# One recurrence head's norm: token sums in nine columns, one small root, and rows made by a product with the identity

## The chip, the cores and the metric

The kernel runs on one core of one Trainium2 chip. The metric is the device time of one launch in microseconds (us). A core has five engines that run their own instruction lists and wait for each other by semaphores: TensorE (PE, with its weight loads PEld), VectorE (DVE), ScalarE (ACT), GpSimd (POOL) and SyncE (SP, which here only issues transfers).

## The reference, cut to what matters

One layer of a hybrid decoder over 1024 prompt tokens and 64 sample tokens. Three head groups read the same normalised input. The change is in group B, a gated linear recurrence with four heads of 128 value features. After the recurrence each token's 128 values of a head are divided by their root mean square, and then gated:

```python
o, S = hgrn2_scan(q, k, v, log_f, S0)            # o: (B, L, 4 heads, 128)
o = o * lax.rsqrt(jnp.mean(o * o, axis=-1, keepdims=True) + EPS)
o = o.reshape(B, L, HGRN_WIDTH) * onorm_g * jax.nn.silu(g)
```

So the norm needs one number for each of 1088 tokens and 4 heads: 4352 inverse roots.

## The kernel before, in words

Activations lie feature by feature: a tile has 128 features on the partitions and the 1088 tokens (1024 prompt, 64 sample) along the free axis. Tokens are cut into three slices `CH` of 364, 362 and 362 columns. Large products are made of three passes over split operands (lines 282 to 284: high part by high, high by low, low by high). They are called projection products here; eight input tiles make 24 of them for one slice of one output tile, and `project` yields after each 6.

The input projections are cut in seven groups (`FIRST`, `WIN[0]` to `WIN[5]`). From `WIN[0]` on, `weave` runs a group's projection steps and, between them, the steps of one head's recurrence, the generator `hgrn(h)`: while the projections for head h+1 stand on PE, head h is worked off. `weave` is told how many steps a head has (`HS`), and spreads so many over the group. With head 3 the cross-attention (`xattn`) and after it the pooling mixer (`pool_mix`) are woven in too. The order in which instructions stand on an engine is then made by a scheduler from the program's order, the pools' free buffers and its own estimates.

The pools matter here: `bank(...)` takes one of four PSUM banks, `tmp(...)` one of seven scratch tiles, `hrow` one of nine half rows.

In `hgrn(h)` the norm stands behind the head's output `o` (line 781; lines 789 and 791 make it, line 798 the 64 sample columns, ACT copies at lines 792 and 800). For each slice (lines 803 to 813): ACT squares it (line 807), a product with a matrix of ones (line 809) sums over the 128 partitions and gives the same sum on each of them, so that the result is already a row by token, equal on all partitions. Then `rsqrt` works on the whole 128x364 tile: mean plus EPS (line 256), an integer shift and subtraction for a first guess (lines 258, 259) and three Newton steps, each a square on ACT (line 250) and two DVE instructions (lines 251, 252). Line 812 multiplies `o` by it. Behind the norm, line 822 makes the sample states' update (`Us`), and line 824 writes them out; then `g_evac` gates `o` (lines 832 to 836).

The kernel has small roots elsewhere. `token_sums` (line 293) takes 128 tokens as the stationary operand, in four strips of 32 columns side by side, and one column of ones as the moving one, so that the sums stand by token on the partitions, in one column. `rstd_last` (line 314) brings such a column back to a row: the column, repeated 128 times, is the stationary operand, and the identity the moving one (line 334).

After these stages come the output projection (lines 953 to 955), the up projection with the convolution (lines 1230 to 1232) and the down projection (lines 1381 to 1383).

Of the kernel before, what the change touches and what calls it, by code (L numbers as in the profile page):

```python
# [15 lines left out]
ALU = mybir.AluOpType  # L16
# [14 lines left out]
CH = [(0, 364), (364, 726), (726, 1088)]  # L31
# [19 lines left out]
def trunk(ctx, tc, I, O):  # L51
# [21 lines left out]
    mm = nc.tensor.matmul  # L73
    act = nc.scalar.activation
    tt = nc.vector.tensor_tensor
# [3 lines left out]
    def row(name, cols=1106, p=128):  # L79
        return rowp.tile([p, cols], F32, tag="row", name=name, bufs=RB)  # L80
# [4 lines left out]
    def tmp(name, cols=None, dt=F32):  # L85
        return now["wk"].tile([128, cols or now["cols"]], dt, tag="tmp", name=name, bufs=now["tmps"])
# [4 lines left out]
    def work(name, tag, bufs, cols, dt=F32):  # L91
        return now["wk"].tile([128, cols], dt, tag=tag, name=name, bufs=bufs)

    def bank(name, shape):
        if now["name"] == "down":
            return acc(name, shape)
        return now["psB"].tile(shape, F32, tag="b", name=name)

    def acc(name, shape):
        return now["psA"].tile(shape, F32, tag="a", name=name)  # L100
# [67 lines left out]
    ident = cst[:, C_ID:C_ID + 128]  # L168
    ones = cst[:, C_ONE:C_ONE + 128]
# [76 lines left out]
    def newton(y, v, a, small):  # L246
        if small:
            tt(out=a, in0=y, in1=y, op=ALU.mult)
        else:
            act(out=a, in_=y, func=AF.Square)  # L250
        stt(out=a, in0=a, scalar=-0.5, in1=v, op0=ALU.mult, op1=ALU.mult)
        stt(out=y, in0=a, scalar=1.5, in1=y, op0=ALU.add, op1=ALU.mult)


    def rsqrt(ss, dim, y, v, a, small=False):
        ts(out=v, in0=ss, scalar1=1.0 / dim, scalar2=EPS, op0=ALU.mult, op1=ALU.add)
        yi = y.bitcast(I32)
        ts(out=yi, in0=v.bitcast(I32), scalar1=1, scalar2=None, op0=ALU.logical_shift_right)
        ts(out=yi, in0=yi, scalar1=-1.0, scalar2=MAGIC, op0=ALU.mult, op1=ALU.add)
        for _ in range(3):  # L260
            newton(y, v, a, small)
# [31 lines left out]
    def token_sums(out, x, start=True, stop=True):  # L293

        for c in range(0, 128, 32):
            mm(out[c:c + 32], x[:, c:c + 32], ones[:, 0:1], start=start, stop=stop, tile_position=(0, c))
# [122 lines left out]
    def head_rows(h):  # L419
        if h not in FR:  # L420
            FR[h], KR[h] = row(f"f{h}", NT), row(f"K{h}", NT)
        QR[h], VR[h] = row(f"Q{h}", NT), row(f"V{h}", NT)
# [4 lines left out]
    for c in range(3):  # L427
        a, b = CH[c]
# [251 lines left out]
    def hgrn(h):  # L680
        f, K, Q, V = FR[h], KR[h], QR[h], VR[h]
# [13 lines left out]
        for half in range(2):  # L695
            tp = bank(f"vtp{h}{half}", [128, 4, 128])
            for i in range(4):
                n = 4 * half + i
# [9 lines left out]
        for li, b in enumerate(LEVELS):  # L708
# [12 lines left out]
            else:  # L721
                nj = 64 // b
                ps = bank(f"sc{h}_{b}", [128, 8, b])
                for n in range(8):
                    for j in range(nj):
                        s0 = 2 * j * b
                        mm(ps[s0:s0 + b, n, :], K[:, n * 128 + s0:n * 128 + s0 + b], Qo[:, n, j, :],
                           start=True, stop=True)
# [8 lines left out]
            if b == 16:  # L737
                for j in range(4):
                    c = slice(32 * j, 32 * j + 32)
# [13 lines left out]
        for hf in range(2):  # L753
            Kt = hrow(f"Kt{h}{hf}").rearrange("p (n v) -> p n v", n=4)
            tp = bank(f"ktp{h}{hf}", [128, 4, 128])
            for i in range(4):
                n = 4 * hf + i
# [7 lines left out]
            for i in range(4):  # L765
                n = 4 * hf + i
# [14 lines left out]
        o = row(f"o{h}", NT)  # L781
# [3 lines left out]
        for hf in range(2):  # L785
            ps = bank(f"o{h}{hf}", [128, 4, 128])
            for i in range(4):
                n = 4 * hf + i
# [7 lines left out]
        for b in range(8):  # L796
            for c in range(0, 128, 32):
                mm(ps[c:c + 32, b, :], s0[b // 4][:, b % 4, c:c + 32], Q[:, NP + 8 * b:NP + 8 * b + 8],
                   start=False, stop=True, skip_group_check=True, tile_position=(0, c))
        act(out=o[:, NP:NT], in_=ps, func=AF.Copy)  # L800
        yield

        for c in range(3):
            a, b = CH[c]
            n = b - a
            sq = tmp(f"osq{h}{c}")
            act(out=sq[:, 0:n], in_=o[:, a:b], func=AF.Square)
            ss = bank(f"oss{h}{c}", [128, n])
            mm(ss, ones, sq[:, 0:n], start=True, stop=True)
            y, v, t = tmp(f"oy{h}{c}"), tmp(f"ov{h}{c}"), tmp(f"ot{h}{c}")  # L810
            rsqrt(ss, 128, y[:, 0:n], v[:, 0:n], t[:, 0:n])
            tt(out=o[:, a:b], in0=o[:, a:b], in1=y[:, 0:n], op=ALU.mult)
            yield

        for hf in range(2):
# [42 lines left out]
    def units(lst, chunk_major=False):  # L858
# [4 lines left out]
        return [lambda nm=nm, j=j, c=c: project(nm, j, c, EV[nm](j)) for nm, j, c in o]  # L863

    hg = [hgrn(h) for h in range(4)]
    HS, XS, PS = 20, 31, 9
    head_rows(1)
    FR[2], KR[2] = row("f2", NT), row("K2", NT)
    weave(units(WIN[0]), (hg[0], HS))
# [727 lines left out]
    a, b = NQ, 2 * NQ  # L1597
# [84 lines left out]
def build(arrays):  # L1682
    nc = bacc.Bacc("TRN2", target_bir_lowering=False, num_devices=1)
    I = {k: nc.dram_tensor(f"in_{k}", a.shape, mybir.dt.from_np(a.dtype), kind="ExternalInput").ap()
         for k, a in arrays.items()}
    O = {k: nc.dram_tensor(f"out_{k}", s, F32, kind="ExternalOutput").ap() for k, s in OUTS.items()}
    with tile.TileContext(nc) as tc:
        with ExitStack() as ctx:
            trunk(ctx, tc, I, O)
    return nc  # L1690
# [27 lines left out]
```

## Time and profile before

| what | value |
|---|---|
| median of 3 runs | 1228.74 us (1227.69 to 1230.68) |
| the profiled execution, its own time | 1228.64 us |
| its span, first to last instruction | 1226.9 us |
| PE busy in the span | 1192.4 us (97%) |
| DVE busy | 925.3 us (75%) |
| ACT busy | 545.4 us (44%) |
| POOL busy | 260.9 us (21%) |

The span is the part that the trace shows; 1.7 us of the execution's time lie around it. A matrix product of the program that is not split by hand appears as two PE records (two passes), a transpose as one. PE's records are pipelined and overlap: a record of 0.33 us is followed by the next after 0.17 us, so the cost of a product is read from start to start. A busy PE is PE with something in flight, not PE at its peak. [...] `q8 instruction` in the table of transfer queues are loads of instructions.

### The profile page before, as it was taken

What the parts mean: (1) busy time and instruction counts of PE and PEld (TensorE: products, weight loads), DVE (VectorE), ACT (ScalarE), POOL (GpSimd) and SP (SyncE); (2) the same over time, 40 slices, a digit from 0 to 9 for tenths busy, and PEclk for the clock granted to TensorE, in tenths of its full rate; (3) what the DMA queues carried; (4) which work ended last, traced back from release to release, by engine and by line L of the source; (5) the groups of instructions that cost most, each with busy time, mean ns of one, the idle gap of its engine ahead of it and who ended that gap; (6) DMA issues with size and microseconds to landing.
All of it is one profiled execution on the core that took longest, in us unless ns stands there. A gap on an engine that the chain in (4) does not pass through costs nothing.

```text
span 1226.9 us, 27524 instructions
## 1 busy us (share of the span) xinstructions
PE 1192.4 (97%) x11332; PEld 1148.2 (94%) x11332; DVE 925.3 (75%) x1675; ACT 545.4 (44%) x1044; POOL 260.9 (21%) x297
## 2 busy tenths in 40 slices
PE   6999999999999999899999999999999999999996
PEld 6999898978878899899999999999999999999996
DVE  7685869487877458989779878987786969868534
ACT  7743534223455455743333332333333445554542
POOL 0000000000000001445454554544323000100242
PEclk9999999999999999999999999999999999999998
DMA  8031111223102643213454354344212597345333
GB/s 270 27 121 53 37 53 53 78 79 120 39 23 91 236 135 115 89 61 132 146 191 139 107 173 159 119 157 158 89 53 70 190 333 263 90 128 151 96 97 111
DMA packets 75838, 148.20 MB, mean 121 GB/s; under 512 B 9264, under 2 KB 31280, under 8 KB 75712
## 3 DMA queue, kind: packets, MB, share of 16 engines
q1 hardware_dynamic: 71776, 140.73, 34.9%
q0 software_dynamic: 1568, 5.39, 1.2%
q8 instruction: 89, 1.46, 0.5%
q10 hardware_dynamic: 2368, 0.32, 0.2%
q14 instruction: 37, 0.30, 0.1%
HBM read 110.48 MB, written 35.93 MB: 119 GB/s over the span
## 4 chain that ended last, share of the span: by engine, by line
PE 59%; DVE 8%; issue 3%; ACT 1%; POOL 0%; DVEq 0%; ACTq 0%; POOLq 0%
PE po L955 2%; PE po L953 2%; PE po L954 2%; PE uUa L1232 2%; PE pV L1381 2%; PE pV L1382 2%; PE pV L1383 2%; PE uUa L1230 2%; PE pP L1381 2%; PE pP L1382 2%; PE uUa L1231 2%; PE uPa L1232 2%; PE pP L1383 2%; PE pU L1381 2%; PE uPa L1230 2%
## 5 line engine op out<-in xcount | busy, mean ns | idle before, releaser
L1369 DVE TENSOR_TENSOR dlp<-drp,dhp 128x512 fp32r<-128x512 f32 x77 | 54.2, 712 | 35.3 <-ACT dhp L1368 34.3
L1368 ACT ACTIVATE dhp<-drp 128x512 fp32r<-128x512 f32 x77 | 47.7, 626 | 69.8 <-PE pU L1382 21.2
L1348 DVE TENSOR_TENSOR xop<-B,xop 128x544 fp32r<-128x544 f32 x70 | 50.0, 729 | 11.6 <-ACT xop L1374 11.6
L1374 ACT ACTIVATE xop<-B 128x544 fp32r<-128x544 f32 x70 | 43.9, 648 | 25.1 <-DVE xop L1348 13.0
L1381 PE MATMUL pU<-xop,dhp 128*128 128x272 f32 x176 | 50.8, 288 | 0.1
L1382 PE MATMUL pU<-xop,dhp 128*128 128x272 f32 x176 | 50.7, 288 | 0.0
L1382 PE MATMUL pV<-xop,dhp 128*128 128x272 f32 x176 | 50.7, 288 | 0.0
L1381 PE MATMUL pV<-xop,dhp 128*128 128x272 f32 x176 | 50.6, 288 | 0.0
L1383 PE MATMUL pV<-xop,dlp 128*128 128x272 f32 x176 | 50.6, 287 | 0.0
L1383 PE MATMUL pU<-xop,dlp 128*128 128x272 f32 x176 | 50.5, 287 | 0.0
L1193 DVE TENSOR_TENSOR g<-g,uc 128x272 f32<-128x272 f32 x66 | 46.1, 699 | 0.8
L1263 ACT ACTIVATE g<-g 128x1104 f32<-128x1104 f32 x22 | 24.8, 1128 | 40.8 <-DVE g L1262 40.8
L1260 DVE SCALAR_TENSOR_TENSOR g<-a,vec,g 128x1104 f32<-128x1104 f32 x22 | 31.8, 1444 | 14.5 <-ACT g L1258 14.5
L1166 POOL TENSOR_TENSOR us0a<-ura 128x512 f32<-128x512 f32 x11 | 18.9, 1718 | 106.3 <-DVE ow160l L925 86.5
L1381 PE MATMUL pP<-xop,dhp 128*128 128x272 f32 x144 | 41.4, 288 | 0.0
L1382 PE MATMUL pP<-xop,dhp 128*128 128x272 f32 x144 | 41.4, 288 | 0.0
L1383 PE MATMUL pP<-xop,dlp 128*128 128x272 f32 x144 | 41.4, 287 | 0.0
L1262 DVE SCALAR_TENSOR_TENSOR g<-a,vec,g 128x1104 f32<-128x1104 f32 x22 | 39.6, 1802 | 0.0
L1266 DVE TENSOR_TENSOR g<-g,ra 128x560 f32<-128x560 f32 x22 | 36.9, 1676 | 0.0
L824 POOL DMA_DIRECT2D out_sstate<-s x8 | 4.3, 541 | 139.9 <-DVE s L823 139.9
L1381 PEld LDWEIGHTS pU<-xop,dhp 128*128 128x128 f32 x176 | 33.1, 188 | 0.3 <-DVE xd L1500 0.3
L1383 PEld LDWEIGHTS pU<-xop,dlp 128*128 128x128 f32 x176 | 33.2, 188 | 0.0
(2313 smaller groups left out, 5053.5 us busy)
## 6 DMA issues: line engine op xcount, KB each, us to landing
ds<-in_wdown SPq DMA_DIRECT2D x44, 256.0 KB, 3.1
ura<-in_wup SPq DMA_DIRECT2D x22, 512.0 KB, 4.4
urb<-in_wup SPq DMA_DIRECT2D x22, 512.0 KB, 3.5
sd<-ds SPq DMA_DIRECT2D x44, 256.0 KB, 2.0
drp<-sd SPq DMA_DIRECT2D x44, 256.0 KB, 2.8
fd<-g SPq DMA_DIRECT2D x20, 544.0 KB, 3.9
B<-fd SPq DMA_DIRECT2D x40, 272.0 KB, 5.6
drp<-in_wdown SPq DMA_DIRECT2D x33, 256.0 KB, 3.2
```

What stands on the lines that cost most here:

```text
L1193: tt(out=dst, in0=dst, in1=s_, op=ALU.mult)
L1230: mm(ps, wh[:, w], xh[:, k], start=first and k == 0, stop=False, skip_group_check=True)
L1232: mm(ps, wl[:, w], xh[:, k], start=False, stop=k == 3, skip_group_check=True)
L1262: stt(out=cw[:, 0:1104], in0=aw[:, 0:1104], scalar=col(V_CW, 3 * f), in1=cw[:, 0:1104], op0=ALU.mult, op1=ALU.add)
L1266: tt(out=tail, in0=tail, in1=ra[0], op=ALU.mult)
L1348: tt(out=out, in0=in0, in1=in1, op=ALU.subtract)
L1368: act(out=wh, in_=raw, func=AF.Copy)
L1369: tt(out=wl, in0=raw, in1=wh.bitcast(F32), op=ALU.subtract)
L1374: act(out=t[:, 0], in_=x, func=AF.Copy)
L1381: mm(ps, w[0][:, c], h, start=start, stop=False, skip_group_check=True)
L1382: mm(ps, w[0][:, c], l, start=False, stop=False, skip_group_check=True)
L1383: mm(ps, w[1][:, c], h, start=False, stop=stop, skip_group_check=True)
```

## The change

The three slices' squares stay on ACT. Their sums are taken by `token_sums`: nine groups of 128 tokens (three to a slice, the last of each overlapping the one before), each one column of a 128x9 PSUM tile. One `rsqrt` with `small=True` then runs on 128x9 for the whole head: twelve DVE instructions, the Newton squares among them (line 248), and none on ACT. Three products per slice, with the repeated column as the stationary and the identity as the moving operand, put the roots back as a row over the tokens, now in PSUM, and the multiplication reads them there. The generator has two more yields, and `HS` goes from 20 to 22.

```diff
@@ -800,16 +800,27 @@
         act(out=o[:, NP:NT], in_=ps, func=AF.Copy)
         yield
 
+        ss = bank(f"oss{h}", [128, 9])
         for c in range(3):
             a, b = CH[c]
             n = b - a
             sq = tmp(f"osq{h}{c}")
             act(out=sq[:, 0:n], in_=o[:, a:b], func=AF.Square)
-            ss = bank(f"oss{h}{c}", [128, n])
-            mm(ss, ones, sq[:, 0:n], start=True, stop=True)
-            y, v, t = tmp(f"oy{h}{c}"), tmp(f"ov{h}{c}"), tmp(f"ot{h}{c}")
-            rsqrt(ss, 128, y[:, 0:n], v[:, 0:n], t[:, 0:n])
-            tt(out=o[:, a:b], in0=o[:, a:b], in1=y[:, 0:n], op=ALU.mult)
+            for i, t in enumerate((0, 128, n - 128)):
+                token_sums(ss[:, 3 * c + i:3 * c + i + 1], sq[:, t:t + 128])
+        y, v, t = [work(f"o{i}{h}", "head", 3, 9) for i in "yvt"]
+        yield
+        rsqrt(ss, 128, y, v, t, small=True)
+        yield
+        for c in range(3):
+            a, b = CH[c]
+            n = b - a
+            yb = bank(f"ob{h}{c}", [128, n])
+            for i, t in enumerate((0, 128, n - 128)):
+                lo = 128 * i
+                mm(yb[:, lo:t + 128], y[:, 3 * c + i:3 * c + i + 1].to_broadcast([128, 128]), ident[:, lo - t:128],
+                   start=True, stop=True)
+            tt(out=o[:, a:b], in0=o[:, a:b], in1=yb, op=ALU.mult)
             yield
 
         for hf in range(2):
@@ -863,7 +874,7 @@
-    HS, XS, PS = 20, 31, 9
+    HS, XS, PS = 22, 31, 9
```

The functions that it calls are in the kernel already:

```python
def token_sums(out, x, start=True, stop=True):
    for c in range(0, 128, 32):
        mm(out[c:c + 32], x[:, c:c + 32], ones[:, 0:1], start=start, stop=stop, tile_position=(0, c))
```

On every engine the instructions stand as before up to the first head's recurrence and from the output projection on; between them they are moved. SP's list changes by the places of six issues, POOL's not at all. Three places follow. In the rows, a name is the tile, with a number for the buffer, and `x12` counts equal rows that follow each other. Lines behind the change are 11 higher in the changed kernel (833 is 822, 831 is 820).

The first is DVE in head 0, from the arrival of the first sums. Before (`ov`, `oy`, `ot` are the root's tiles, `f<-pf` the evacuation of the next head's projection):

```order
L256 TENSOR_SCALAR ov_1591<-oss_1588 128x364
L258 TENSOR_SCALAR oy_1590<-ov_1591 128x364
L259 TENSOR_SCALAR oy_1590<-oy_1590 128x364
L401 TENSOR_TENSOR f_960<-pf_1532,R_128 128x364
L251 SCALAR_TENSOR_TENSOR ot_1592<-ot_1592,ov_1591 128x364
L252 SCALAR_TENSOR_TENSOR oy_1590<-ot_1592,oy_1590 128x364
L256 TENSOR_SCALAR ov_1629<-oss_1626 128x362
```

And now:

```order
L401 TENSOR_TENSOR f_960<-pf_1486,R_128 128x364
L256 TENSOR_SCALAR ov_1611<-oss_1567 128x9
L258 TENSOR_SCALAR oy_1610<-ov_1611 128x9
L259 TENSOR_SCALAR oy_1610<-oy_1610 128x9
L248 TENSOR_TENSOR ot_1612<-oy_1610 128x9
L251 SCALAR_TENSOR_TENSOR ot_1612<-ot_1612,ov_1611 128x9
L252 SCALAR_TENSOR_TENSOR oy_1610<-ot_1612,oy_1610 128x9
L248 TENSOR_TENSOR ot_1612<-oy_1610 128x9
```

The wide root, which stood between other work slice by slice, has become one chain of narrow instructions behind the evacuation of a projection slice. On PE in this place, the sums stand 6 projection products behind the sample columns of line 798, the first identity products 24 projection products behind the sums.

The second is PE in head 3, where the attention's sample products (`so`, line 614) and the sample columns (`os`, line 798) come together with the norm. Before:

```order
L798 MATMUL os_3950<-Q_2444,s_30_3867 32x8 x9
L614 MATMUL so<-spT,svt_3914 32x16 x16
L798 MATMUL os_3950<-Q_2444,s_30_3867 32x8 x7
L798 MATMUL os_3950<-Q_2444,s_31_3868 32x8 x16
L614 MATMUL so<-spT,svt_3985 32x16 x16
L809 MATMUL oss_4012<-osq_4010,cst 128x364
L614 MATMUL so<-spT,svt_4030 32x16 x16
L284 MATMUL pg_4003<-h4h,wlo_3263 128x362
```

And now:

```order
L798 MATMUL os_3953<-Q_2470,s_30_3899 32x8 x9
L614 MATMUL so<-spT,svt_3929 32x16 x16
L798 MATMUL os_3953<-Q_2470,s_30_3899 32x8 x7
L798 MATMUL os_3953<-Q_2470,s_31_3900 32x8 x16
L614 MATMUL so<-spT,svt_3988 32x16 x16
L296 MATMUL oss_4012<-cst,osq_4013 32x1 x12
L296 MATMUL oss_4012<-cst,osq_4027 32x1 x12
L296 MATMUL oss_4012<-cst,osq_4041 32x1 x12
L614 MATMUL so<-spT,svt_4082 32x16 x16
L284 MATMUL pg_4100<-h3h,wlo_3302 128x362
L614 MATMUL so<-spT,svt_4112 32x16 x16
L282 MATMUL pg_4100<-h4h,whi_3301 128x362
```

All 36 sums stand in a run of small products, with no projection product between line 798 and them. The identity products of head 3 follow 20 projection products and these last two groups of `so` later.

The third is PE a little later, at the first scores of the attention (`xs`) and the first transposes of its probabilities (`xtp`, from `xp`). In the kernel before, 36 projection products (`pu`) stand between the last of the first eight `xs` and the first `xtp`. Now there are 11, of which these are the last four, and all eight transposes stand together:

```order
L284 MATMUL pu_4242<-h4h,wlo_3808 128x364
L282 MATMUL pu_4242<-h5h,whi_3807 128x364
L283 MATMUL pu_4242<-h5l,whi_3807 128x364
L284 MATMUL pu_4242<-h5h,wlo_3808 128x364
L647 MATMUL xtp_4270<-cst,xp_4182 128x128 x4
L647 MATMUL xtp_4276<-cst,xp_4183 128x128 x4
L282 MATMUL pu_4242<-h6h,whi_3807 128x364
```

The first probabilities are asked for 25 projection products sooner.

## Rows read from the trace of the kernel before

**Rows 1.** The page, part 1: busy time, share, instructions.
```profile
PE 1192.4 (97%) x11332; PEld 1148.2 (94%) x11332; DVE 925.3 (75%) x1675; ACT 545.4 (44%) x1044; POOL 260.9 (21%) x297
```

**Rows 2.** Stretches: length, busy PE, PEld, DVE, ACT, POOL; clock, DMA share, GB/s.
```profile
125.00:150.00 25.00, 25.00 (x266) 21.94 (x265) 22.33 (x48) 12.11 (x26) 1.08 (x2) 1.00 0.13 45
```

**Rows 3.** Waits of PE: total us, times, longest (whole span; these lie before 403 us).
```profile
PE po L953 <- DVE sg L835: 1.9, 1, 1.9
PE so L614 <- issue: 1.7, 1, 1.7
...
PE po L955 <- DVE ow000l L925: 0.6, 1, 0.6
...
PE xs L631 <- DVE s L823: 0.2, 1, 0.2
```

**Rows 4.** The wide root by line: ns min/median/max, first and last start.
```profile
L256 DVE TENSOR_SCALAR ov<-oss x12: 525/536/539, 126.9 to 318.8; 128x362 f32<-128x362 f32 x8, 128x364 f32<-128x364 f32 x4
...
L258 DVE TENSOR_SCALAR oy<-ov x12: 340/349/381, 127.4 to 320.3; 128x362 int32<-128x362 int32 x8, 128x364 int32<-128x364 int32 x4
...
L251 DVE SCALAR_TENSOR_TENSOR ot<-ot,ov x36: 522/530/539, 128.7 to 329.0; 128x362 f32<-128x362 f32 x24, 128x364 f32<-128x364 f32 x12
...
L250 ACT ACTIVATE ot<-oy x36: 489/506/511, 128.2 to 328.4; 128x362 f32<-128x362 f32 x24, 128x364 f32<-128x364 f32 x12
```

**Rows 5.** Timeline of PE around two products of line 809: start, us, instruction.
```profile
125.89 0.33 PE L284 MATMUL pf<-h5h,wlo 128*128 128x362 f32 x1
126.06 0.77 PE L809 MATMUL oss<-osq,cst 128*128 128x364 f32 x2
126.39 0.60 PE L282 MATMUL pf<-h6h,whi 128*128 128x362 f32 x1
126.83 0.32 PE L283 MATMUL pf<-h6l,whi 128*128 128x362 f32 x1
...
128.99 0.32 PE L284 MATMUL pf<-h2h,wlo 128*128 128x362 f32 x1
...
130.05 0.33 PE L283 MATMUL pf<-h3l,whi 128*128 128x362 f32 x1
```

**Rows 6.** Timeline of PE, unsplit 128-column products behind each other.
```profile
119.74 0.39 PE L791 MATMUL o<-Q,S 128*128 128x128 f32 x2
119.96 0.39 PE L789 MATMUL o<-scT,Vt 128*128 128x128 f32 x2
```

**Rows 7.** Timeline of PE: token sums of another norm, and what follows.
```profile
56.16 0.37 PE L296 MATMUL n12ss<-cst,n12s 128*32 128x1 f32 x24 [0.34 <-DVE n12s L311]
56.45 0.43 PE L282 MATMUL pi<-h0h,whi 128*128 128x362 f32 x1
56.73 0.33 PE L283 MATMUL pi<-h0l,whi 128*128 128x362 f32 x1
```

**Rows 8.** Timeline of DVE: a Newton step of a small root.
```profile
1218.06 0.16 DVE L248 TENSOR_TENSOR nf10t<-nf10y 128x3 f32<-128x3 f32 x1
1218.26 0.16 DVE L251 SCALAR_TENSOR_TENSOR nf10t<-nf10t,nf10v 128x3 f32<-128x3 f32 x1
```

**Rows 9.** Timeline of ACT at head 3: the copy of the sample columns.
```profile
305.20 0.22 ACT L800 ACTIVATE o<-os 128x64 f32<-128x64 f32 x1 [1.15 <-PE os L798]
```

**Rows 10.** Timeline of DVE: one step of the attention's softmax.
```profile
342.15 0.69 DVE L562 TENSOR_REDUCE x20mx<-xs 128x2 f32<-128x512 f32 x1
...
345.76 0.62 DVE L568 TENSOR_SCALAR xp<-xp,x21sm 128x256 f32<-128x256 f32 x2
```

**Rows 11.** Timeline of PE inside head 3's run of small products.
```profile
304.95 0.38 PE L614 MATMUL so<-spT,svt 128*32 128x16 f32 x21
307.02 0.27 PE L614 MATMUL so<-spT,svt 128*32 128x16 f32 x10 [1.69 <-issue]
```

**Rows 12.** The page, part 3: loads of instructions (packets, MB, share).
```profile
q8 instruction: 89, 1.46, 0.5%
```

**Rows 13.** Stretches behind that wait, columns as in rows 2.
```profile
309.00:311.00 2.00, 2.00 (x7) 2.00 (x8) 1.17 (x4) 1.66 (x6) 0.00 (x0) 0.50 0.34 31
```

## The prediction

> **What bounds the kernel now.** I read the totals first: PE is busy 97% of the span, DVE 75%, ACT 44% [rows 1]. A total says little about one stage, so next come the stretches in which the norm runs. From 125 to 150 us PE is busy all of the time; DVE is busy 22.33 of 25, and much of that is the wide root of head 0 [rows 2]. A busy PE may still be a PE that waits between overlapping records, so third I read start to start: projection products of 362 columns follow each other at 0.17 us on both sides of the norm's products [rows 5], and that is the pace to compare with. Fourth, the waits of PE before 403 us [rows 3]: 1.9 and 0.6 at the start of the output projection, 1.7 inside the attention's sample products, 0.2 at the first scores. No line waits for the root. So in the head stages PE carries the time, and the reader is to see that DVE and ACT run beside it: what the change takes from DVE is worth little, and what it adds to PE is paid.
>
> **What leaves DVE and ACT.** By slice one instruction of 0.536, two of 0.349, six of 0.53, and three ACT squares of 0.506; for twelve slices 6.4 + 8.4 + 38.1 = 53 us of DVE and 18 us of ACT [rows 4]. In come 48 narrow instructions; the nearest, on three columns, last 0.16 [rows 8], so 7.7 us of DVE. The multiplication by a row in PSUM I take at the same cost as before. Net 45 us of DVE. I cost this at nothing: PE's products cover it, and the cover is gone only where PE waits for DVE, which sums to 0.2 us outside the output projection's start [rows 3]. That start hangs on the gating of the last projection slice, whose instructions stand as before.
>
> **What PE pays.** (1) Removed: twelve products of line 809. The first stretches the way from 125.89 to 126.83, in which two projection products would take 0.33, so it costs 0.61; the second, from 128.99 to 130.05, costs 0.73 [rows 5]. Mean 0.67, times twelve 8.0 us, bounds 7.3 and 8.8. (2) Added: three identity products for each slice, 364 columns together. An unsplit product of 128 columns takes 0.22 start to start [rows 6], so 0.63 a slice and 7.5 us in all. The projection product after a change of kind takes 0.28 instead of 0.17 [rows 7]; the removed products have that in their 0.67, so I add 0.11 for each of the ten places where the identity products stand: 8.6 us, bounds 7.5 and 8.9. So the way back to a row costs what the wide sum cost. (3) Added: 36 sums for each head, 72 passes. The same operation in another norm took 0.29 us for 24 passes [rows 7], so 0.87 for a head, 3.5 for four, and 3.9 with four changes of kind. Net of the three: +4.5 us, bounds 2.2 (7.5 + 3.5 - 8.8) and 5.5 (8.9 + 3.9 - 7.3).
>
> [...] Each pass takes 0.29 / 24 = 0.012 us [rows 7]. [...]
>
> **The waits that it moves.** (4) The sums of the third slice need its square, which follows the copy of the sample columns: 0.22 [rows 9] and 0.51 on ACT [rows 4], from the end of line 798. In heads 0 to 2 PE has 6 projection products (1.0) and the sums of two slices (0.58) meanwhile; the 0.85 left covers the handing over, so nothing; without cover 0.7 a head. In head 3 there is no projection product between, and up to 0.5 is lost, but I expect it to fall inside wait (7). What stands behind a PE that waits is the next projection, and nobody else needs that soon. (5) The identity products need the whole chain: twelve narrow instructions at 0.20 start to start [rows 8], 2.4, behind an evacuation of 0.54, so 2.9 against 24 projection products, 4.0. Nothing in heads 0 and 1, and head 2 has as many between. In head 3 the cover is 20 products and two groups of small ones, some 3.9; the chain shares DVE with four wide instructions of other work, some 2.2, so 4.6. I take 0.2 of the 0.7, since the clock may be low there, which lengthens the cover; bounds 0 and 0.7. (6) The first transposes come 25 projection products sooner. Both halves of a softmax step took 4.2 us from the first reduction [rows 10], and one more reduction (0.69) now stands among them: 4.9. The cover is four score products of 256 columns, 1.75 by the rate of [rows 6], eleven projection products, 1.8, and the first half's four transposes, one pass each, 0.45: 4.0. Of the 0.9 I take 0.7, and the old 0.2 at the scores goes away: +0.5, bounds -0.2 and 0.9. (7) In head 3 PE stops for 1.69 us in the middle of a group of equal small products, released by nothing that the profile shows [rows 11]. PE's 22664 records [rows 1] go with 89 instruction loads of 16 KB [rows 12], 255 records to a load, so I read this as a list that ran dry: small products use up a load faster than the next one arrives. The change puts 144 more records (36 sums, two passes, each with a weight load) into just this run. Bounds: nothing, since the position in a load shifts too, and one more stop of 1.7. I take +0.4, near the first, since the stop's length goes by the load's delay and not by the run's.
>
> [...] The rows alone give 255 records a load [rows 1, 12]. [...]
>
> The transfers stay whole; of SP's list six issues change place, with their neighbours. One matters: all loads of the sample values (`svt`) now stand behind the load of `chist`, which waits for head 3's masks. Their first use comes later on PE too, so I take nothing.
>
> **Sum.** 4.5 + 0.2 + 0.5 + 0.4 = 5.6 us on the profiled execution's 1228.64, so 1234.2 us. That execution lies 0.1 below the median shown.
>
> **Rivals.** *A second stop.* [...] With 1.6 for some 3 us of low clock a second stop costs 3.3: 1237.5. For it: 144 records more than before; against it: projection products come right behind. *No measurable change.* The same stop disappears, since the loads' borders shift by 504 records in three heads, and the low clock with it: 0.4 falls away and 3.3 is won, so 1230.5. For it: such a stop is seen at one place alone; against it: head 3's run is longer than a load now, wherever the border falls. *Faster.* PE's full busy share in the head stages hides small waits for DVE that no row names, and 45 us less of DVE takes them away. For it: DVE is near full from 125 to 150 [rows 2]. Against it: the 0.17 start to start next to the norm [rows 5], at which nothing is hidden. It decides from 9.3 us of hidden waits on (5.6 + 3.7); were a quarter of the 45 us on PE's path, 11 us, the time would be 1223. *Dear sums.* The sums cost twice what the other norm's rows show, since they stand among other kinds of product: 3.7 more, 1238. [...]
>
> **How the numbers follow.** The forecast case (1232.5 to 1236.5) has 0.55, the second stop 0.12, the dear sums 0.03, no change 0.25, faster 0.05. 1234.2 is the likeliest case's. The range of 1229.5 to 1238.5 takes in the lost stop, the second one and the dear sums, and leaves out the faster case and some of the edges. 0.3% of the median is 3.7 us, about what a measurement of this kernel can tell from no change; over 1232.4 is slower: 0.55 + 0.12 + 0.03 = 0.70, same 0.25, faster 0.05.
>
> **What would show it.** Line 296 with 288 more passes, at 0.012 us start to start; line 821 with 72 passes, 0.63 us a slice; DVE some 45 us less busy and the span longer all the same; the stop in head 3's small products still there, 1.7 to 2.5 us; a wait of the first `xtp` for the probabilities under 1 us; the wait at the output projection's start unchanged at 1.9. The prediction is wrong if the projection products of the head stages come closer together than 0.17 us over a whole stage, if the stop is gone, or if a wait of several us for the root appears in each head, which would say that a narrow instruction costs far more than 0.20.

## The result and the profile after

The changed kernel takes 1235.11 us (median of 4 runs, 1234.22 to 1236.55), the kernel before beside it 1228.22: a ratio of 1.0053 (95% interval 1.004 to 1.0065). Its profiled execution took 1234.81, with a span of 1233.0. The forecast was 1234.2, slower; the time lies in the range. How it came to 6 or 7 us is not quite how the prediction had it.

The totals of the page after, to be read against [rows 1] and [rows 12]:

```profile
PE 1196.0 (97%) x11668; PEld 1154.0 (94%) x11668; DVE 888.9 (72%) x1615; ACT 530.6 (43%) x1008; POOL 261.4 (21%) x297
...
q8 instruction: 91, 1.49, 0.5%
```

DVE is 36 us less busy, ACT 15, and the kernel is longer. The waits of PE after (total, times, longest), against [rows 3]:

```profile
PE po L966 <- DVE ow170l L936: 2.7, 1, 2.7
PE oss L296 <- issue: 2.1, 1, 2.1
PE po L964 <- ACT ow000h L935: 1.9, 1, 1.9
...
PE po L964 <- ACT ow170h L935: 1.3, 1, 1.3
PE xo L655 <- ACT xt L648: 1.3, 3, 0.8
...
PE po L966 <- DVE ow000l L936: 0.6, 1, 0.6
...
PE xtp L647 <- DVE xp L568: 0.6, 1, 0.6
```

The stop without a releaser is there (2.1, was 1.7), the first transposes wait 0.6, the start of the output projection waits 1.9 and 0.6 as before. New are 1.3 us of `xo` in the attention and, near the end of the output projection, 1.3 of `ow170h` and 0.5 more of `ow170l` (2.2 before), in code that the change doesn't touch.

The sums and the rows on PE in head 0 (timeline: start, us, instruction), against [rows 5]:

```profile
122.27 0.33 PE L284 MATMUL pf<-h7h,wlo 128*128 128x364 f32 x1
122.53 0.78 PE L296 MATMUL oss<-cst,osq 128*32 128x1 f32 x72
123.24 0.43 PE L282 MATMUL pf<-h0h,whi 128*128 128x362 f32 x1
123.51 0.33 PE L283 MATMUL pf<-h0l,whi 128*128 128x362 f32 x1
...
127.17 0.33 PE L284 MATMUL pf<-h7h,wlo 128*128 128x362 f32 x1
127.34 0.81 PE L821 MATMUL ob<-cst,oy 128*128 128x128 f32 x6
127.92 0.41 PE L282 MATMUL pf<-h0h,whi 128*128 128x362 f32 x1
128.17 0.33 PE L283 MATMUL pf<-h0l,whi 128*128 128x362 f32 x1
```

From 122.27 to 123.51 are 1.24 us, of which two projection products would take 0.33: 0.91 for a head's 36 sums. From 127.17 to 128.17, 1.00 less 0.33: 0.67 for a slice's row. A wide sum cost 0.67 in [rows 5].

The next two fences are the timeline of the stop in head 3, and the stretches behind it (columns as in [rows 2]):

```profile
306.21 0.42 PE L296 MATMUL oss<-cst,osq 128*32 128x1 f32 x29
308.72 0.75 PE L296 MATMUL oss<-cst,osq 128*32 128x1 f32 x42 [2.09 <-issue]
```

```profile
308.00:310.00 2.00, 1.28 (x76) 1.24 (x75) 0.44 (x2) 0.34 (x1) 0.00 (x0) 0.50 0.00 0
...
312.00:314.00 2.00, 2.00 (x9) 2.00 (x8) 0.61 (x4) 0.10 (x1) 0.00 (x0) 0.50 0.77 59
```

The stop stands in the middle of the sums, and the granted clock, a share of the full one, is at 0.50 until beyond 314; in [rows 13] it is low too, but from 312 on the kernel before has 1.00. At 0.50 projection products of 362 columns follow each other at 0.30 us (nine from 311.83 to 314.54 in the changed kernel), 1.8 times the 0.17 at 1.00.

**The account.** The table parts each trace in the same way. "Head stages" runs from the 301st projection product (81.4 us before), ahead of any norm, to the first product of the output projection; 1140 projection products at 0.1665 us (189.8) are taken off, and the rest is parted into what PE waited (start to start, 0.1 to 0.2 more for each than the view of waits says), what the low clock cost (start to start, against the same products at full clock), and all other work. "Output" is first to last product of that projection, "rest" from there to the last PE record.

| kernel | head stages | other work | waits | low clock | output | rest |
|---|---|---|---|---|---|---|
| before | 320.2 | 123.5 | 5.0 | 1.9 | 103.4 | 714.4 |
| changed | 324.6 | 125.3 | 6.9 | 2.6 | 107.0 | 713.0 |
| e1 first guess | 316.2 | 122.4 | 4.0 | 0 | 104.9 | 712.9 |
| e2 sums twice | 331.3 | 127.8 | 9.3 | 4.4 | 103.5 | 714.9 |
| e3 rows twice | 331.8 | 132.8 | 7.5 | 1.7 | 103.5 | 715.0 |
| e4 one pass | 317.2 | 118.7 | 6.9 | 1.8 | 106.7 | 714.2 |
| e5 one pass, HS 21 | 312.7 | 120.0 | 2.9 | 0 | 105.4 | 713.4 |
| e6 head 3 old | 318.8 | 126.7 | 2.3 | 0 | 101.8 | 715.3 |
| e7 changed again | 324.2 | 125.3 | 6.6 | 2.5 | 107.0 | 713.2 |
| e8 unsplit sums | 328.1 | 129.7 | 4.6 | 4.0 | 103.3 | 715.2 |
| e9 28 more products | 316.6 | 124.3 | 2.5 | 0 | 107.6 | 714.4 |
| e10 44 more products | 318.4 | 124.6 | 4.0 | 0 | 106.2 | 713.9 |
| e11 changed, HS 20 | 322.3 | 125.9 | 6.6 | 0 | 106.6 | 713.2 |
| e12 changed, 24 more | 324.7 | 125.4 | 7.2 | 2.3 | 106.2 | 713.5 |

So the change is +1.8 of work, +1.9 of waits and +0.7 of low clock in the head stages, and +3.6 - 1.4 behind them. That is 6.6; the spans differ by 6.1, since the time behind PE's last record is 0.5 shorter. e7 repeats it to 0.5. Output and rest are best read as a sum, since a low clock that the kernel before has at the start of the up projection (behind a wait of 1.6 there) comes ahead of that border in the changed one: 817.8 before, 820.0 after. Each trace is one execution: those of e8 and e12 are the slowest of their six (3.4 and 2.3 us above the median), and one run of e4, at 6527 us, is left out of its ratio.

### The profile page after: what moved, and what is told of

It is laid out like the page before. It is cut to its first block, busy times and chain, and to the rows that moved or that the text cites. A ratio compares the mean times of both kernels' runs of the same rounds, so it can differ in the third digit from the quotient of the medians.

```text
span 1233.0 us, 28095 instructions
## 1 busy us (share of the span) xinstructions
PE 1196.0 (97%) x11668; PEld 1154.0 (94%) x11668; DVE 888.9 (72%) x1615; ACT 530.6 (43%) x1008; POOL 261.4 (21%) x297
## 4 chain that ended last, share of the span: by engine, by line
PE 78%; DVE 12%; issue 4%; ACT 3%; DMA 2%; SPq 0%; DVEq 0%; POOL 0%; ACTq 0%; POOLq 0%
PE po L966 2%; PE po L964 2%; PE po L965 2%; PE pP L1392 2%; PE pP L1393 2%; PE pP L1394 2%; PE pU L1392 2%; PE pU L1393 2%; PE pU L1394 2%; PE uPa L1243 2%; PE uVa L1241 2%; PE uPa L1241 2%; PE uUa L1243 2%; PE uPa L1242 2%; PE uUa L1242 2%
## 5 line engine op out<-in xcount | busy, mean ns | idle before, releaser
L213 ACT ACTIVATE whi<-raw 128x1024 fp32r<-128x1024 f32 (+1 forms) x24 | 24.5, 1022 | 38.5 <-PE px L283 14.0
L1392 PEld LDWEIGHTS pV<-xop,dhp 128*128 128x128 f32 x176 | 33.1, 188 | 0.3 <-DVE xd L1511 0.3
```

The costliest lines, as they stand in the source:

```text
L1392: mm(ps, w[0][:, c], h, start=start, stop=False, skip_group_check=True)
```

## The experiments

**What PE is charged: e1 to e3.** e1 takes the relief without the products (`steps` is 0 in `hgrn` and 3 elsewhere):

```diff
-        for _ in range(3):
+        for _ in range(steps):
             newton(y, v, a, small)
```

> The kernel before, with its wide root cut to the first guess: the three Newton steps (36 ACT squares, 72 DVE instructions on 128x362) are left out, so the roots are rough. PE's products stay as they were, all twelve wide sums included; DVE has some 38 us less to do and ACT 18 us less, about the relief that the change brings, without its products. My theory (PE carries the head stages, and DVE and ACT run beside it): 1226 to 1230 us, the projection products still 0.166 to 0.17 apart. Rival (part of DVE's work lies on PE's path unnamed, a quarter of the 56 us): 1213 to 1220 us.

Measured: 1224.93 us, ratio 0.9977 (0.9966 to 0.9987), between the two. The waits of PE up to the output projection's start:

```profile
PE po L953 <- ACT ow000h L924: 1.9, 1, 1.9
PE xo L655 <- ACT xt L648: 1.3, 3, 0.9
...
```

The stop is gone (1.9 from start to start), and with it 1.9 of low clock. The waits of `xo` are new, so that the waits are 1.0 less in all, and the other work is 1.1 less: 4.0 together in the head stages. The run is not the relief alone, since the scheduler moved more than a tenth of PE's records to another place; but 56 us less of DVE and ACT gained 2.9 us in all, the stop and its clock among them. That the stop could vanish with no product removed was unexpected, and e9 takes it up.

e2 and e3 issue the added products twice:

```diff
-                token_sums(ss[:, 3 * c + i:3 * c + i + 1], sq[:, t:t + 128])
+                for _ in range(2):
+                    token_sums(ss[:, 3 * c + i:3 * c + i + 1], sq[:, t:t + 128])
```

> The changed kernel, with every group of token sums issued twice (the second overwrites the first): 288 more passes on PE, nothing else. The changed kernel's 288 passes took 3.0 us without their stop. My theory: +3.0 us, 1238 us; with a further stop for instructions in head 3's run, which grows by 144 more records, up to 1240. [...] Rival that the products added are hidden and the loss comes from the order alone: 1235 us.

> The changed kernel, with every identity product issued twice (the second overwrites the first): 72 more passes on PE, 24 of 362 columns together for each of the twelve slices, nothing else. In the changed kernel a pass of 128 columns takes 0.11 us and the shorter ones 0.09. My theory: +7.5 us (0.63 a slice), 1242.6 us. Rival that the way back to a row is hidden behind other waits of PE: 1235 to 1237 us.

e2: 1239.79 us, 1.0095 (1.0079 to 1.011). Its other work is 2.5 more than the changed kernel's, and head 3 has two stops, shown here; a third, of 1.0 us, stands in head 1's sums at 182 us. The low clock costs 4.4, behind all three:

```profile
PE oss L296 <- issue: 2.6, 1, 2.6
PE so L614 <- issue: 1.6, 1, 1.6
```

e3: 1240.94 us, 1.0108 (1.0095 to 1.0122). Its other work is 7.5 more, as expected; read start to start, the second set costs 0.67 in each of the nine slices of heads 0 to 2, which would be 8.1 for twelve. In both, output and rest together give 1.5 us back, so the times come out below what work and waits add. Nothing of the added products is hidden; the second set of sums costs 2.5 / 288 = 0.009 us a pass.

**A cheaper wide sum: e4 and e5.** The same root, with one pass for its sum:

```diff
-            sq = tmp(f"osq{h}{c}")
+            if h == 0 and c == 0:
+                act(out=onesr, in_=ones[:, 0:2], func=AF.Copy)
+            sq = tmp(f"osq{h}{c}", dt=F32R)
...
-            mm(ss, ones, sq[:, 0:n], start=True, stop=True)
+            mm(ss, onesr[:, 0:1].to_broadcast([128, 128]), sq[:, 0:n], start=True, stop=True)
```

> The kernel before, with the wide root kept and only its sum made cheaper: ACT writes the squares rounded to the operand format of the projection products, and each of the twelve products with the ones is one pass of 362 columns in place of two. My theory (the time goes by PE's products alone): each of the twelve costs 0.17 to 0.28 us in place of 0.67, so 4.7 to 6.0 us less: 1222.2 to 1223.5 us. Rival (the sum on PE is not what counts here, DVE's root is): 1228 us.

1228.94 us, 1.0008 (0.9999 to 1.0018): no gain. Its timeline around a sum:

```profile
126.53 0.33 PE L285 MATMUL pf<-h5h,wlo 128*128 128x362 f32 x1
126.70 0.34 PE L812 MATMUL oss<-osq,onesr 128*128 128x364 f32 x1
126.88 0.33 PE L283 MATMUL pf<-h6h,whi 128*128 128x362 f32 x1
```

The product costs 0.18 here, 0.23 in the mean of eight that stand alone, and the other work is 4.8 less, as the theory has it. But the wait at the output projection's start went from 1.9 to 3.4 and the one behind it from 0.6 to 1.9:

```profile
PE po L956 <- ACT ow000h L927: 3.4, 1, 3.4
...
PE po L958 <- DVE ow000l L928: 1.9, 1, 1.9
```

With the cheaper product the scheduler had moved the eight splits `c` of the output projection's operands: on DVE six of them stand behind the last evacuation `gz` and ahead of the split `ow000l`. Before the first of the eight DVE idles 3.8 us for ACT, but 4.3 in e5 too. In the kernel before none stands there. e5 changes only `HS` to 21, by which two stand there (its expectation says ahead where it should say behind):

> The kernel before with the one-pass sum of e4 and HS at 21, which puts the splits of the output projection's operands behind head 3's gating, nearly as in the kernel before; e4 had them ahead of it. In e4's trace PE's work up to the output projection was 4.8 us shorter than before, and waits and low clock from there on gave 3 to 5 us back. Theory (the saving on PE is real and e4 lost it to the order of the last 20 instructions on DVE and ACT): 1222.5 to 1225 us, with the first wait of the output projection at 1.9 to 2.0 and not 3.5. Rival (the end of the projections is bound by DVE and ACT whatever the order, so PE's saving is lost there): 1228 to 1229 us, and the wait grows by what PE gains.

1221.51 us, 0.9945 (0.9932 to 0.9958), faster than both kernels. The waits up to that start:

```profile
PE po L957 <- DVE sg L839: 1.7, 1, 1.7
PE po L959 <- DVE ow000l L929: 1.1, 1, 1.1
PE so L615 <- issue: 0.4, 1, 0.4
```

Against the kernel before, the gain is 3.5 of work, 1.3 of the stop and the whole of its low clock. The kernel before with `HS` at 21 and the old sum was not run. So it is not shown how the gain divides between the cheaper sum and the new order, nor how much the end of DVE's work would have cost e4 in any order.

**Where the loss sits: e6, e7, e8.** e6 is the changed kernel with the old block under `if h == 3`, and `HS` 20 for that head.

> The changed kernel, with head 3's norm as in the kernel before (HS 20 for it); heads 0 to 2 keep the new norm. Theory (of the loss, head 3's group holds more than its share: the longer stop, its low clock and the waits of the transposes and of the second products of the attention, 3 us more than before; its products cost 0.9 net): against the changed kernel -0.9 for the products, -3.5 for stop, clock and waits, +1.0 because the score products stand among the attention's other products again: 1231.7 us. Rival (each head loses the same by its products, 6.9 / 4): 1233.4 us.

1228.18 us, 0.9991 (0.9981 to 1.0002): three heads of four have the new norm, and the time is that of the kernel before. Its waits from 250 us to the end of the output projection:

```profile
PE po L979 <- DVE ow170l L949: 2.1, 1, 2.1
...
PE xo L655 <- ACT xt L648: 0.2, 1, 0.2
```

The three heads cost 3.2 us of work (three quarters of the 4.5 forecast are 3.4), but no stop is left, and no low clock. So both theories missed: neither had the stop of the kernel before go as well. In this trace the output projection has no low clock either, by which it is 1.6 shorter than before.

e7 is the changed kernel as it is.

> The changed kernel once more, for a second trace and more times. In the first trace the output projection took 107.1 us, in the kernel before 103.5, in e2 and e3, which have the same instructions there, 103.6. If those 3.6 us come of how its transfers happened to fall, the output projection's time will differ from 107.1 in this trace; if the changed kernel has them always, it is 107 again. The time: 1234.5 to 1235.5 us either way.

1234.61 us, 1.0051 (1.0039 to 1.0063); the output projection took 107.0 again. The 3.6 us belong to the kernel.

e8 takes the 128 tokens in one product:

```diff
-                token_sums(ss[:, 3 * c + i:3 * c + i + 1], sq[:, t:t + 128])
+                mm(ss[:, 3 * c + i:3 * c + i + 1], sq[:, t:t + 128], ones[:, 0:1], start=True, stop=True)
```

> The changed kernel with the sums of 128 tokens in one product on all 128 columns in place of four strips of 32: 9 products a head and not 36, the same sums. By the stop's theory (PE's list runs dry because small products use it up faster than it is loaded) head 3's run has 27 products, 108 records, less, and the stop of 2.25 us gets shorter or goes: -1 to -3 us with its low clock. The passes themselves cost between 0.05 and 0.11 us each, 18 a head: 0.9 to 2.0 in place of 0.9. Sum 1232 to 1236 us. Rival (the stop has nothing to do with the number of instructions): the stop stays at 2.2 us, 1235 to 1239 us.

1235.17 us, 1.0057 (1.0042 to 1.0073), no faster than the changed kernel. The stop is gone (a wait of 0.7 for a transfer of `svt` stands near its place), and the sums are dearer: other work is 4.4 more. Head 0, timeline:

```profile
123.82 0.33 PE L284 MATMUL pf<-h7h,wlo 128*128 128x364 f32 x1
123.99 2.06 PE L810 MATMUL oss<-cst,osq 128*128 128x1 f32 x18
125.91 0.41 PE L282 MATMUL pf<-h0h,whi 128*128 128x362 f32 x1
126.16 0.33 PE L283 MATMUL pf<-h0l,whi 128*128 128x362 f32 x1
```

2.34 less 0.33 is 2.01 for 18 passes, 0.11 each against 0.91 / 72 = 0.013 in strips.

**Why the stop comes and goes: e9, e10, e11.** e9 and e10 leave the kernel before as it is, and put products whose result is overwritten ahead of head 0's first sum, 180 us before the stop (seven groups of four in e9, eleven in e10):

```diff
+            if h == 0 and c == 0:
+                for _ in range(7):
+                    token_sums(ss[:, 0:1], sq[:, 0:128])
             mm(ss, ones, sq[:, 0:n], start=True, stop=True)
```

> The kernel before, with 28 more small products (seven groups of token sums, 112 PE instructions) ahead of head 0's first wide sum, which overwrites what they write. Every other instruction on every engine stands as before, and so does head 3's run, some 180 us later. Theory (the stop in head 3 comes where the border of a load of 256 instructions falls, and two loads can't follow each other in less than about 3.5 us): shifted by 112 places no load is used up in less than 3.5 us, so the stop of 1.9 us and the low clock behind it, 1.85, are gone, for 0.7 us of added products: 1225.5 us. Rival (the stop belongs to the run of small products itself, wherever the loads' borders fall): it stays, 1229 us.

> As e9, with 44 more small products (176 PE instructions), the control. Theory: a border now falls so that one load of head 3's run lasts about 2 us, so a stop of 1.5 to 1.9 us stays there with its low clock: 1229 to 1230 us. Rival (any shift or any delay takes the stop away): 1225.7 us.

Waits of PE from 250 to 405 us, e9:

```profile
PE po L956 <- DVE sg L838: 1.9, 1, 1.9
...
PE xs L631 <- DVE s L826: 0.2, 1, 0.2
```

The stop is gone in e9, where on PE nothing differs but the position in the list, and in e10 it is there, with 1.0 us, less than the 1.5 to 1.9 expected, and no low clock behind it. In the trace's records of instruction loads, the loads on either side of the stop begin at 304.65 and 308.27 us in the kernel before, 3.62 apart, and at 306.48 and 310.08 in the changed one, 3.60; nowhere in the fourteen traces do two follow in less than 3.29. So a load that is used up faster stops PE, and whether one is depends on where its border falls in head 3's run.

The traces tie the stops to the loads by two more counts. They have 19 stops without a releaser, of 0.2 to 2.6 us, and each ends 2.2 to 2.9 us after the start of a load. And if all of PE's records (products, weight loads, semaphores) are counted from 0, the one with which PE goes on has in all 19 cases the remainder 193 when divided by 256: 7873 in the kernel before, 8385 in the changed one. The prediction took such a stop for one at a single place. The kernel before has another, in the waits of PE over the whole span:

```profile
PE sc L677 <- issue: 0.5, 1, 0.5
```

It ends at 96.62 us, with record 1729. A run that is longer than a load need not stop, though: e9 has head 3's run and no stop.

The time of e9 is 1229.71 us, though, 1.0016 (1.0007 to 1.0025), not 1225.5: it was 3.8 us ahead at the output projection and lost 4.2 in it, so the rival's 1229 is met for another reason than the rival's. e10: 1228.31, 1.0002 (0.9993 to 1.0011).

> The changed kernel with HS at 20 as before: the same instructions, in another order in the head stages. Counting instructions in loads of 256, head 3's run has one load of 3.1 us in it and none shorter. Theory (the products cost the same whatever the order, and the rest of the loss hangs on where the stop falls): the stop shrinks from 2.25 to about 0.4 us and its low clock of 2.4 goes, so 4 us less than the changed kernel, 1230.5 to 1231.5 us, with at most 1 us of waits more or less in the attention. Rival (the loss is the products' alone): 1235 us.

1232.21 us, 1.0034 (1.0021 to 1.0046). This is 2.4 below e7, not 4. There is no stop in head 3 (0.4 was expected) and no low clock. The waits in the attention are 1.0 more than the changed kernel's (1.4 and 0.2 at `ob` come, 0.6 at `xtp` goes, `xo` keeps its 1.3), and the wait for `ow170h` is there too.

**The output projection: e12.** In four traces (changed, e7, e9, e11) PE waits for `ow170h`, and in no other. What they share is a load of PE's instructions among the transfers 76 to 82 us after that projection's start, begun within 1.9 us of the second store of `x1d`, ahead of it or behind. e10 has a load at 76.9 too, but 2.8 us ahead of that store, which landed in 3.0 us. Seven us of the transfer view in the changed kernel, then the same place in the kernel before:

```profile
q1 hardware_dynamic: 688, 1.08, 48.3%
q8 instruction: 1, 0.02, 0.8%
...
x1d<-xb SPq DMA_DIRECT2D x2, 272.0 KB, 3.8
```

```profile
q1 hardware_dynamic: 688, 1.08, 46.5%
...
x1d<-xb SPq DMA_DIRECT2D x2, 272.0 KB, 2.7
```

The last column is the median of the two stores `x1d`; the second one lands after 4.2 us in place of 3.0. ACT, which overwrites the stored row, goes on that much later, and with it `T2h` and DVE. DVE in the changed kernel, then before:

```profile
490.91 1.29 DVE L1020 TENSOR_TENSOR T2l<-xb,T2h 128x1088 fp32r<-128x1088 f32 x1 [0.99 <-ACT T2h L1029]
492.12 1.79 DVE L936 TENSOR_TENSOR ow160l<-or,ow160h 128x512 fp32r<-128x512 f32 x1
493.82 2.37 DVE L1020 TENSOR_TENSOR B11l<-xb,B11h 128x1088 fp32r<-128x1088 f32 x1
```

```profile
485.49 1.29 DVE L1009 TENSOR_TENSOR T2l<-xb,T2h 128x1088 fp32r<-128x1088 f32 x1
486.70 0.69 DVE L925 TENSOR_TENSOR ow160l<-or,ow160h 128x512 fp32r<-128x512 f32 x1
487.33 1.29 DVE L1009 TENSOR_TENSOR B11l<-xb,B11h 128x1088 fp32r<-128x1088 f32 x1
```

One us late, and `ow160l` and `B11l` fall into POOL's sums of up weights, which begin here in the changed kernel (in the kernel before at 487.45, when `B11l` had begun):

```profile
491.95 1.40 POOL L1177 TENSOR_TENSOR us0a<-ura 128x512 f32<-128x512 f32 x1 [86.60 <-DMA ura<-in_wup]
```

Beside these they take 1.1 us more each (1.79 for 0.69, 2.37 for 1.29); the splits into `ow170h` and `ow170l` end 1.3 and a further 0.5 us later for PE. In the kernel before it is the next split, `ow161l` at 488.54, that stands beside POOL's first sum (487.45 to 489.78) and takes 1.78; what the two engines share there is not shown. e12 moves the border by 96 places:

> The changed kernel, with 24 more small products (96 PE instructions) ahead of head 0's first token sums, which overwrite what they write; nothing else stands otherwise. In the four traces whose output projection took 106.6 to 107.6 us with a wait for ow170h (the changed kernel twice, e9, e11), a load of PE's instructions began 76 to 81 us after that stage's start, among the transfers of the first up weights and of the stored rows, and the second of these stores took 4.1 to 4.9 us; in the others no load fell there, or the store came later, and it took 2.7 to 3.0. Theory (a load of instructions in the way of that store makes the 3.5 us): shifted by 96 places the load comes at about +71 us, the store takes 3.0 us, the wait for ow170h is gone and the stage takes 103.4 us; the stop in head 3 stays above 2 us. Time 1233 to 1234 us (1.6 less in the later stages, 0.6 more for the products). Rival (it belongs to the changed kernel in some other way): 107 us again, 1235.2 us.

The load came at +72.8 us, and the wait for `ow170h` is gone. The transfer view of the same place, then the waits of PE from 250 to 515 us:

```profile
x1d<-xb SPq DMA_DIRECT2D x2, 272.0 KB, 2.6
```

```profile
PE so L614 <- issue: 2.5, 2, 1.5
PE po L969 <- DVE ow170l L939: 2.1, 1, 2.1
...
```

The theory holds for the store, the wait and the stop, which stays (2.5). The stage took 106.2 us, not 103.4: behind the waits at its start and for `ow170l`, which are no longer than before, the low clock cost 4.4 here and 1.5 before. At the start the clock is at 0.50 from 407.9 to 414.7 us, before from 403.4 to 406.8. So output and rest together are 819.7, against 820.0 in the changed kernel: the load is shown to make the late store and the wait, and what it costs in the end is not shown. e10 has 820.1 there without that wait. The time is 1233.46 us, 1.0033 (1.0021 to 1.0045), where it was expected, but its interval overlaps the changed kernel's, and the trace is of an execution of 1235.78.

## Why the prediction came out right, step by step

- **PE carries the head stages, and relief of DVE and ACT is worth nothing.** Held, as far as e1 shows it: it gained 2.9 us, and the stop and its clock are 3.8. DVE fell by 36 us and not 45: its durations overlap the next by 0.08 us (1.29 long, 1.21 apart in the last fence of DVE), so durations add up to more than busy time. For the time this is nothing.
- **Terms 1 to 3.** Removed 8.0 forecast; eight wide sums that stand alone cost 0.673 each (0.60 to 0.88), so 8.1. Rows 8.6, measured 12 x 0.666 = 8.0, e3 7.5. Sums 3.9, measured 4 x 0.905 = 3.6, e2 2.5 for the second set. Net 3.5 in place of 4.5. This is the term of the sum that was mis-sized: the change of kind was charged on top at 0.11, of which 0.03 to 0.04 showed in each place. In the rows even that may be the products' own, since e3's second set, with no change of kind, costs 0.67 a slice as well.
- **What the sum left out.** All other work in the head stages grew by 1.8, not by 3.5. Where the order moved, small products of other work shared their changes of kind differently: a step of the attention cost 4.07 us before, as one group of 16 `xo`, 4 `xs` and 8 `xtp`, and 3.87 in four groups after, 1.0 for five steps. The other 0.7 I have not placed.
- **Term 4, the sums wait for the square.** Nothing in heads 0 to 2, as forecast.
- **Term 5, the chain of the root.** 0.2 forecast, no wait of `ob` seen (e11, in another order, has 1.4 for ACT and 0.2 for the root).
- **Term 6.** `xtp` waits 0.6 (0.7 forecast), the 0.2 of `xs` is gone. The nearness says little for this sum: four score products take 1.06 us (338.56 to 339.62 in the trace after), not the 1.75 in its cover. Missed: 1.3 us of `xo` for ACT's copies of the transposes, the next link of the same chain, three times in the steps as they now stand. The steps behind the first were not looked at. e1 has the same 1.3 with none of the new products, so these alone do not make it; the order in which the steps stand is the likelier cause, which was not tried by itself.
- **Term 7, the stop.** +0.4 forecast and +0.4 measured, and the reading of it as a list that runs dry is shown by e9 and by the 19 borders. What was not priced is that the clock stays low longer: +0.7.
- **The stages behind, taken as unchanged.** This is the step that failed: +2.2 us net. The instructions are the same, but 672 more PE instructions ahead of them put a load among transfers, which makes 1.8 of waits (`ow170h` and `ow170l`); the wait of `uPa` at the start of the up projection is 0.9 less (0.7, was 1.6). The rest lies in small waits and the low clock, which moves between executions of these stages: with the load shifted, e12's trace has 1.9 of the 2.2 still. That the load makes the whole of it is not shown.
- **The rivals.** A second stop did not come in the changed kernel; it came in e2, with 1.6 us (priced at 1.7) and at most 0.7 more of low clock in head 3 (priced at 1.6; of e2's 4.4, at least 1.1 lie behind its third stop, at 182 us). The 1.6 for some 3 us of low clock was an estimate; in the kernel before, 3.4 us of it (307.8 to 311.2) cost 1.9. "No measurable change" named the right lever: in e9 the stop vanishes by a shift. Its objection held too, since in the changed kernel the stop survived the shift of e12. "Faster" fell with e1, "dear sums" with e2: no run shows its 3.7, and a pass of e2's second set costs 0.009 us, less than the 0.012 of [rows 7].

So the total is near because savings that were missed (1.0 of grouping, 1.0 of products, 0.7 not placed) and losses that were missed (1.3 at `xo`, 0.7 of clock, 2.2 behind) nearly cancel. That PE pays for the products and that the stop stays were right by the mechanism; that the sum of the terms came within 1 us is luck.

## What to carry to other kernels

Where PE is full, price a rewrite by PE alone: moving a norm's root from 128x362 to 128x9 took 36 us from DVE and put 3.5 us of products on PE, while taking one pass out of the same sum gained 0.55% in one order (e5, of which 3.5 us is work on PE) and nothing in another (e4). A change in the number of instructions shifts every later load of instructions, so a loss or gain of 2 to 4 us can show 200 us behind the edit, in code that stands as before; padding of a few products, as in e9, changes the position alone: there 3.8 us came and 4.2 went. And a saving on PE is kept only if the chain that ends the stage, here the last gating and its splits, is not put later by the new order (e4).

## What the hardware did that I had not expected

- A load of 16 KB of PE's instructions among transfers made a 272 KB store land after 4.1 to 4.9 us in four traces, after 2.7 to 3.0 in the ten others. With the load shifted ahead by 7.0 us of the store (e12) it landed after 2.8, with 2.8 us between them (e10) after 3.0; on which of the DMA engines the load sits was not looked at.
- The wait at the output projection's start (1.9 us in twelve traces, 3.4 in e4, 1.7 in e5) was followed by a clock of 0.50 in thirteen traces and not in e6; in e4, e10 and e12 the clock stayed low about twice as long as in the other ten. The stretches behind the wait in the kernel before, then in e6:

```profile
403.00:405.00 2.00, 2.00 (x11) 2.00 (x12) 0.41 (x1) 0.00 (x0) 0.00 (x0) 0.60 1.02 417
```

```profile
402.00:404.00 2.00, 2.00 (x18) 2.00 (x17) 0.06 (x1) 0.00 (x0) 0.00 (x0) 1.00 1.00 390
```
